# Softmax of neighbourhood attention fused differently, and weight sums of the v and g projections moved from accumulating DMAs to GpSimd, in a two-layer encoder

## The chip, the cores and the metric

One core of a Trainium2 chip. The metric is the device time of one execution in microseconds (us). Engines: TensorE (PE; weight loads PEld), VectorE (DVE), ScalarE (ACT), GpSimd (POOL), SyncE (SP, which here only issues DMAs).

## The reference, cut to what matters

Two layers over 512 tokens (8 rows of 64 columns) of width 1024, all float32. Each layer: one input projection of x to neighbourhood attention (8 heads of 64), retention (4 heads, q and k of 128, v and g of 256) and gates; then a merge, LayerNorm, a gated feed-forward part and a second LayerNorm. The change lies in the neighbourhood attention and in the projection to v and g:

```python
s = einsum('bhcd,bhrckd->bhcrk', q_row, k_win) * scale   # window: 8 rows x 16 columns
s = s + bias                                             # na_rpb at row and column offset
pr = softmax(s over the window's 128 keys)
out = einsum('bhcrk,bhrckd->bhcd', pr, v_win)
...
proj = x @ w_in[i]      # q_na, k_na, v_na, q_r, k_r, v_r, g_r, gate_a, gate_b
yb = silu(g_r) * groupnorm(retention(q_r, k_r, v_r))
```

## The kernel before, in words

**Matmuls.** Every float32 product is three matmuls on a split operand: `hi` is the value cast to fp32r on ScalarE, `lo` is value minus `hi` on VectorE (`split`, lines 157 and 158; `mm3`, lines 372 to 374). Each weight goes through this: a DMA brings 128x1024 (`raw`, 512 KB), ScalarE makes `hi`, VectorE `lo`, TensorE uses both. `Stream` holds all weights of the program in the order of use; `load` runs `LOOK` = 3 items ahead of `prep` (the split), which runs ahead of `get` (the use).

**The v/g stage.** The columns of v and g are done in two blocks of two heads (0 and 1). In a block the weight is cut into quarters a, b, c, d, and seven products in place of eight are formed, with the sums t1 = a+b, t2 = t1+d, t4 = t2+c and t3 = b+d of packed quarters (the signs are in the packing). `block_items` makes the items a, c, t1, t2, d, t3, t4, two halves each. The raw buffer of a becomes that of t1, t2 and t4 in turn (`nxt`): once one is split, `Stream.add` adds the next quarter to the raw tile (`rawa`) by a GpSimd DMA with accumulation from DRAM. t3 (`rawt`) is loaded as b, with d added in the same way, when the item d is loaded (`early`). So for t2 and t3 the same quarter d is read from DRAM again, besides its own load for the product d. `VG0` and `VG1` give the order of products by hand, with other projections (ga0 to ga3, q0, k0) and, in layer 0, the start-up work between them; `vg_sums` makes the corresponding sums of x (tiles s, sh, sl) on VectorE. GpSimd otherwise issues the accumulating DMAs of other stages, raises variances to the power -0.5, and little else.

**The attention stage.** After v/g, the remaining projections (`FILL`) and gates run as fillers on TensorE, one slot each; retention heads and neighbourhood heads are generators whose steps are put between the fillers by slot numbers (`RET_AT`, `NA_AT`). The framework then orders each engine's instructions; each engine works through its own queue in order. `na_head(h)` has three steps. First step: the window of biases `tb` (128x249) is loaded and, with the mask (0 or -1e30, `mask_sb`), makes the bias B of 128x512, one half for the three inner query tiles, one for the edge tile (line 941); four pairs of matmuls per head give the scores `ns` in two PSUM banks of two query tiles; VectorE adds B into S (lines 958 and 961), takes the maximum over each of the four tiles at once (963), negates it (964); ScalarE does four exponentials with the sum (967); VectorE the reciprocal (970) and four scales (972). Second step: eight transposes of S on TensorE (980) and their split (`pt`). Third: matmuls with `vn`, the split v (992), and copies. `vn` is made by `na_v`, a filler which stands between the heads, from `xc`, a reordered copy of x made on ScalarE (`column_tiles`, line 892) just before.

**Buffers.** `up` is the pool of units of 4 KB per partition that hold S, split operands, raw tiles of a and t3 and much else; there are `N_UNIT` = 27. Plain raw tiles come from a pool of three.

Of the kernel before, what the change touches and what calls it, by code (L numbers as in the profile page):

```python
# [8 lines left out]
F32 = mybir.dt.float32  # L9
F32R = mybir.dt.float32r  # L10
AF = mybir.ActivationFunctionType
ALU = mybir.AluOpType
# [9 lines left out]
LN_EPS = 1e-5  # L22
GN_EPS = 1e-6
ALPHA = (2.0 * DEPTH) ** 0.25
RPB_PAD = 16
RPB_N = 8 * 15 * 31

N_UNIT = 27
N_RAW = 3
N_W = 3  # L30
N_TMP = 6
# [69 lines left out]
    return a.bitcast(F32)  # L101


def trunk(tc, wpack, x_nat, x_tr, head, p_tr, rpb, decay, ln_par, ln_col, conv, cos_t, sin_t, dist, xi_d, zd, mask, ident_d, out):
    nc = _Engines(tc)
    _Ordered.on = set()
    from contextlib import ExitStack
# [1 line left out]
    with ExitStack() as es:  # L109
# [14 lines left out]
        def nm(s):  # L124
            cnt[0] += 1
            return f"{s}_{cnt[0]}"
# [21 lines left out]
        mask_sb = cp.tile([P, 512], F32, name="mask_sb")  # L148
        cos_sb = cp.tile([P, 512], F32, name="cos_sb")
        sin_sb = cp.tile([P, 512], F32, name="sin_sb")  # L150

# [8 lines left out]
        class Item:  # L160
# [7 lines left out]
            def __init__(self, kind, src, width, pool=None, plus=None, own=None):  # L168
                self.kind, self.src, self.width, self.pool, self.plus, self.own = kind, src, width, pool, plus, own
                self.raw = self.hl = None  # L170
                self.nxt = self.early = self.block = None

                self.sent = kind == "w" and any(a <= src[1] < b for a, b in SENT)

        def block_items(pos, held, early):

            out = []
            prev = {}
            for kind, src, plus in (("a", "a", None), ("c", "c", None), ("t1", None, "b"), ("t2", None, "d"),
                                    ("d", "d", None), ("t3", "b", "d"), ("t4", None, "c")):  # L180
                for j in range(2):
                    at = lambda q: None if q is None else pos[q, j]
                    it = Item(kind, at(src), pos["a", j][3], plus=at(plus), own=kind in ("a", "t3"), pool=held.get(kind))
                    if kind in ("a", "t1", "t2", "t4"):
                        if j in prev:
                            prev[j].nxt = it
                        prev[j] = it
                    if kind == "t3":
                        [o for o in out if o.kind == early][j].early = it
                    out.append(it)  # L190
            return out

        def down_items(l, s):
# [16 lines left out]
        def vg_items(l):  # L210

            by = {}
            for b in range(2):
                pos = {(q, j): (l, 12 * b + 2 * i + j, 0, 1024) for i, q in enumerate("acbd") for j in range(2)}
                for it in block_items(pos, {k[1:]: up for k in VG_HELD[l] if k[0] == str(b)}, VG_EARLY):
# [34 lines left out]
        class Stream:  # L250
# [26 lines left out]
                self.late = {}  # L277

            def add(self, it):
                l, c, o, w = it.plus  # L280
                nc.gpsimd.dma_start(it.raw[:, :w], wpack[l, c][:, o:o + w], accum_op=ALU.add)

# [16 lines left out]
            def load(self, n, part=None):  # L299

                while self.nload < min(n, len(self.seq)):
                    it = self.seq[self.nload]
                    if it.src is not None and it.kind != "t3":
                        self.fetch(it, part)
                        if it.early is not None:
                            self.fetch(it.early)
                    self.nload += part != 0
                    if part == 0:
                        return
# [224 lines left out]
        def tables():  # L534
            for t, d in ((cos_sb, cos_t), (sin_sb, sin_t), (xi_sb, xi_d.to_broadcast([P, 512])), (dist_sb, dist), (ident, ident_d)):
                nc.sync.dma_start(t, d)
            yield
            nc.sync.dma_start(mask_sb, mask)
            for h in range(2):
                tbs[0, h] = bp.tile([P, 249], F32, tag="tb", name=nm("tb"))  # L540
# [82 lines left out]
        for l in range(DEPTH):  # L623
# [307 lines left out]

            def na_head(h):
                m, rr = h // 2, (h % 2) * 64
                tb = tbs.pop((l, h), None)
                if tb is None:
                    tb = bp.tile([P, 249], F32, tag="tb", name=nm("tb"))
                    nc.sync.dma_start(tb, rpb[l, h])
                B = bp.tile([P, 512], F32, tag="B", name=nm("B"))
                for o, off, st in ((0, 0, 16), (256, 8, 0)):
                    v3 = lambda x: x[:, o:o + 256].rearrange("p (b r j) -> p b r j", b=2, j=16)  # L940
                    nc.vector.tensor_add(v3(B), _ap(tb, off, [[st, 2], [31, 8], [1, 16]]), v3(mask_sb))
                S = unit_f("S")
                q, k, kw = qn[m], kn[m], kl[m]
                hs = slice(rr, rr + 64)

# [3 lines left out]
                for b in range(2):  # L949
                    ps = bank("ns")  # L950
                    for gi in range(2):
                        g = 2 * b + gi
                        c = slice(g * P, (g + 1) * P)
                        o = ps[:, gi * 256:(gi + 1) * 256]
                        nc.tensor.matmul(o, q[:, h % 2, c], kv(k[:, h % 2, :], g), start=True, stop=False)
                        nc.tensor.matmul(o, q[:, h % 2, c], kv(kw[:, h % 2, :], g), start=False, stop=True)
                    if b == 0:
                        nc.vector.tensor_add(S[:, 0:512].rearrange("p (g n) -> p g n", g=2), ps.rearrange("p (g n) -> p g n", g=2),
                                             _ap(B, 0, [[0, 2], [1, 256]]))
                    else:  # L960
                        nc.vector.tensor_add(S[:, 512:1024], ps, B)
                nmx = small("nmx", 4)
                nc.vector.tensor_reduce(nmx, S.rearrange("p (g n) -> p g n", g=4), axis=AX.X, op=ALU.max)
                nc.vector.tensor_scalar_mul(nmx, nmx, -1.0)
                sm = small("sm", 4)
                for g in range(4):
                    nc.scalar.activation(S[:, g * 256:(g + 1) * 256], S[:, g * 256:(g + 1) * 256], AF.Exp,
                                         bias=nmx[:, g:g + 1], accum_out=sm[:, g:g + 1])
                rc = small("rc", 4)
                nc.vector.reciprocal(rc, sm)  # L970
                for g in range(4):
                    nc.vector.tensor_scalar_mul(S[:, g * 256:(g + 1) * 256], S[:, g * 256:(g + 1) * 256], rc[:, g:g + 1])
# [555 lines left out]

def _rpb_windows(rpb):

    flat = np.pad(rpb.reshape(DEPTH, RPB_N), ((0, 0), (RPB_PAD, RPB_PAD)))
    h = np.arange(8)[:, None, None, None] * 465
    rq = np.arange(8)[None, :, None, None]
    u = np.arange(16)[None, None, :, None]
    idx = RPB_PAD + h + (7 - rq) * 31 + 7 - u + np.arange(249)
    return flat[:, idx.reshape(8, P, 249)]


def _consts():
    half = 64  # L1540
    f = np.float32
    inv = (f(10000.0) ** (-np.arange(half, dtype=f) / f(half))).astype(f)
    ang = np.arange(T, dtype=f)[None, :] * inv[:, None]
    cos, sin = np.cos(ang).astype(f), np.sin(ang).astype(f)
    cos_t = np.concatenate([cos, cos], 0)
    sin_t = np.concatenate([sin, -sin], 0)
    dist = (np.arange(384)[None, :] - np.arange(P)[:, None] - 128).astype(f)
    n = np.arange(T)
    xi = np.where(n < 256, 256 - n, n - 255).astype(f)[None, :]
    zd = np.where(n < 256, 255 - n, n - 256).astype(f).reshape(4, P).T  # L1550
    u = np.arange(P) % 16
    j = np.arange(32)
    vi = (j[None, :] - u[:, None] >= 0) & (j[None, :] - u[:, None] < 16)
    ve = (j[None, :] // 16) == (u[:, None] // 8)
    mk = lambda v: np.tile(np.where(v, 0.0, -1e30).astype(f).reshape(P, 2, 1, 16), (1, 1, 8, 1)).reshape(P, 256)
    mask = np.concatenate([mk(vi), mk(ve)], 1)
    return cos_t, sin_t, dist, xi, zd, mask, np.eye(P, dtype=f)


# [36 lines left out]
```

## Time and profile before

| what | value |
|---|---|
| time, median of 3 runs | 1695.96 us (1695.86 to 1696.27) |
| the profiled execution: span, first to last instruction | 1694.1 us, granted TensorE clock 0.998 |
| median less span (start and end around the instructions) | 1.9 us |
| PE busy | 1680.6 us (99%), 7895 matmuls |
| DVE, ACT, POOL busy | 1227.8 (72%), 923.8 (55%), 146.7 us (9%) |
| moved by DMA | 256.59 MB, mean 151 GB/s |

The profiled execution's own time is its span. In rows of groups the columns are line, engine, operation, output<-inputs, shape, count, then busy us and mean ns of one, then the engine's idle time just before them and what ended it. In rows of the timeline they are start (us), duration (us; of the whole run of instructions where the row has x2 or more), engine, line, operation, names, count, and in brackets idle time with its releaser.

### The profile page before, as it was taken

The page shows a single profiled execution, that of the slowest core. Times are in us where ns is not written, and L with a number is a line of the kernel's source. Part 1 is how long each engine was busy: PE and PEld are TensorE (multiplying, and loading weights), DVE is VectorE, ACT ScalarE, POOL GpSimd, SP SyncE. Part 2 cuts the span into 40 slices and gives each one's busy share as a digit, 9 for nine tenths or more (in the row PEclk, how much of TensorE's full clock was granted, in tenths as well). Part 3 has the DMA queues.
Part 4 walks back from the last instruction along what each step waited for, and adds up shares of the span by engine and source line. Part 5 has one row for each costly group of instructions (what it writes and reads, how often), then busy time and mean ns, then how long its engine had stood idle before and what let it go on. Part 6 is the DMA issues. An engine that isn't in the chain of part 4 may idle for free.

```text
span 1694.1 us, 21018 instructions
## 1 busy us (share of the span) xinstructions
PE 1680.6 (99%) x7895; PEld 1404.1 (83%) x7895; DVE 1227.8 (72%) x1848; ACT 923.8 (55%) x1368; POOL 146.7 (9%) x166
## 2 busy tenths in 40 slices
PE   9999999999999999999999999999999999999997
PEld 7888888888888888888888888888888888888886
DVE  6667767756787767757876677576578887676678
ACT  6755668654367445344476555676534574353452
POOL 1100010000200100100112001100002010000003
PEclk9999999999999999999999999999999999999999
DMA  8954464344655535535779435643456565264275
GB/s 299 259 160 131 112 155 110 108 143 147 190 148 151 123 113 164 136 111 173 201 206 238 124 98 133 150 103 106 147 203 188 135 173 125 88 185 126 87 212 100
DMA packets 76855, 256.59 MB, mean 151 GB/s; under 512 B 8912, under 2 KB 11472, under 8 KB 76752
## 3 DMA queue, kind: packets, MB, share of 16 engines
q1 hardware_dynamic: 58608, 191.27, 32.8%
q0 software_dynamic: 18144, 63.97, 21.7%
q8 instruction: 62, 1.02, 0.2%
q14 instruction: 41, 0.34, 0.1%
HBM read 240.53 MB, written 13.63 MB: 150 GB/s over the span
## 4 chain that ended last, share of the span: by engine, by line
PE 97%; DVE 2%; ACT 1%; issue 0%; DVEq 0%; ACTq 0%
PE gt L87 32%; PE u L87 13%; PE gt L372 8%; PE gt L373 8%; PE gt L374 8%; PE v L87 7%; PE w L87 3%; PE gn L372 3%; PE gn L374 3%; PE gn L373 3%; PE x L87 2%; PE gn L87 1%; PE na L992 1%; PE pt L980 1%; PE o L374 1%; PE o L373 1%
## 5 line engine op out<-in xcount | busy, mean ns | idle before, releaser
L87 PE MATMUL gt<-x1t,hi 128*128 128x512 f32 x1408 | 433.3, 389 | 0.0
L87 PEld LDWEIGHTS gt<-x1t,hi 128*128 128x128 f32 x1408 | 264.3, 188 | 54.6
L87 PE MATMUL gt<-x1t,lo 128*128 128x512 f32 x704 | 274.1, 389 | 0.1
L87 DVE TENSOR_TENSOR lo<-raw,hi 128x1024 fp32r<-128x1024 f32 (+1 forms) x155 | 185.6, 1208 | 45.0 <-ACT hi L87 44.6
L87 DVE SCALAR_TENSOR_TENSOR ca<-gt,cw,ca 128x511 f32<-128x511 f32 x176 | 131.8, 749 | 79.1 <-ACT ca L87 75.6
L87 ACT CAST hi<-raw 128x1024 fp32r<-128x1024 f32 (+1 forms) x155 | 159.3, 1038 | 35.8 <-PE u L87 16.6
L372 PE MATMUL gt<-xt,hi 128*128 128x512 f32 x416 | 163.5, 393 | 0.0
L373 PE MATMUL gt<-xt,hi 128*128 128x512 f32 x416 | 162.2, 390 | 0.0
L374 PE MATMUL gt<-xt,lo 128*128 128x512 f32 x416 | 162.1, 390 | 0.0
L87 PEld LDWEIGHTS gt<-x1t,lo 128*128 128x128 f32 x704 | 132.2, 188 | 28.4 <-DVE lo L87 1.0
L157 ACT CAST hi<-raw 128x1024 fp32r<-128x1024 f32 x72 | 75.6, 1050 | 126.4 <-PE gt L373 65.4
L87 ACT ACTIVATE ca<-gt,cw 128x512 f32<-128x512 f32 x88 | 68.6, 779 | 131.9 <-PE gt L87 131.9
L87 DVE TENSOR_TENSOR lo<-rawa,hi 128x1024 fp32r<-128x1024 f32 x90 | 104.7, 1175 | 42.3 <-ACT hi L87 42.0
L158 DVE TENSOR_TENSOR lo<-raw,hi 128x1024 fp32r<-128x1024 f32 x72 | 88.0, 1222 | 62.4 <-ACT hi L157 62.1
L87 ACT CAST hi<-rawa 128x1024 fp32r<-128x1024 f32 x90 | 90.0, 1013 | 38.3 <-DMA rawa<-in_wpack 19.9
L374 PEld LDWEIGHTS gt<-xt,lo 128*128 128x128 f32 x416 | 78.1, 188 | 16.6
L87 POOL DMA_DIRECT2D rawa<-in_wpack x68 | 61.3, 916 | 338.2 <-DVE lo L87 293.5
L373 PEld LDWEIGHTS gt<-xt,hi 128*128 128x128 f32 x416 | 78.3, 188 | 14.9
L372 PEld LDWEIGHTS gt<-xt,hi 128*128 128x128 f32 x416 | 78.2, 188 | 14.9
L87 PE MATMUL gt<-xt,hi 128*128 128x512 f32 x192 | 59.1, 389 | 0.0
L87 PE MATMUL v<-hi,sa 128*128 128x512 f32 x176 | 56.1, 389 | 0.0
L372 PE MATMUL gn<-hi,mt 128*128 128x512 f32 x128 | 50.2, 392 | 0.0
(324 smaller groups left out, 3600.0 us busy)
## 6 DMA issues: line engine op xcount, KB each, us to landing
raw<-in_wpack SPq DMA_DIRECT2D x247, 512.0 KB, 3.9
rawa<-in_wpack POOLq DMA_DIRECT2D x66, 512.0 KB, 6.3
lo<-in_wpack POOLq DMA_DIRECT2D x24, 512.0 KB, 6.7
rawa<-in_wpack SPq DMA_DIRECT2D x22, 512.0 KB, 6.5
rawt<-in_wpack SPq DMA_DIRECT2D x22, 512.0 KB, 6.8
rawt<-in_wpack POOLq DMA_DIRECT2D x22, 512.0 KB, 7.6
r_scr<-pp SPq DMA_DIRECT2D x8, 512.0 KB, 10.0
g_scr<-sga SPq DMA_DIRECT2D x16, 256.0 KB, 4.0
```

Source lines behind the costliest of these rows:

```text
L87: r = f(*a, **k)
L157: nc.scalar.copy(hi, src)
L158: nc.vector.tensor_sub(lo, src, _f(hi))
L372: nc.tensor.matmul(ps, lh, rh, start=start, stop=False, skip_group_check=more)
L373: nc.tensor.matmul(ps, lh, rl, start=False, stop=False, skip_group_check=more)
L374: nc.tensor.matmul(ps, ll, rh, start=False, stop=stop, skip_group_check=more)
L980: nc.tensor.transpose(ps[:, i * P:(i + 1) * P], S[:, g * 256 + bb * P:g * 256 + (bb + 1) * P], ident)
L992: nc.tensor.matmul(ov[kt], lv, pt[kt // 2][:, sp_, c], start=i == 0 and sp_ == 0, stop=i == 3 and sp_ == 1)
```

## The change

1. In `na_head`, B (bias and mask together, 128x512) comes ready from DRAM: the host's gather puts -1e30 where the mask was. `tb`, `mask_sb` and line 941 go.
2. The two S adds, the maximum and the negation become four fused instructions of 128x256 (one per query tile): S = -(scores + B), with the running minimum as accumulator into `nmx`. The exponential takes scale -1.
3. The four scales by the reciprocal move from VectorE to ScalarE (a Copy with a scale per partition).
4. In the two v/g blocks of both layers, t2 and t3 get d by a GpSimd add of 128x1024 from d's own raw tile, which is now loaded with the first of them that needs it, into a unit buffer (`own`), in place of the accumulating DMA. t1 and t4 keep their DMAs.
5. 30 unit buffers instead of 27, and a scratch area for GpSimd's DMA descriptors of 4096 bytes per partition in place of the default.

```diff
-N_UNIT = 27
+N_UNIT = 30
...
-        def block_items(pos, held, early):
+        def block_items(pos, held, early, onchip=False):
...
+            if onchip:
+                ds = [o for o in out if o.kind == "d"]
+                for it in out:
+                    if it.kind == "d":
+                        it.own = True
+                    if it.kind in ("t2", "t3"):
+                        it.other = ds[len([o for o in out[:out.index(it)] if o.kind == it.kind])]
...
             def add(self, it):
+                if it.other is not None:
+                    if it.other.raw is None:
+                        self.fetch(it.other)
+                    nc.gpsimd.tensor_tensor(it.raw, it.raw, it.other.raw, ALU.add)
+                    return
                 l, c, o, w = it.plus
                 nc.gpsimd.dma_start(it.raw[:, :w], wpack[l, c][:, o:o + w], accum_op=ALU.add)
...
                     if it.src is not None and it.kind != "t3":
-                        self.fetch(it, part)
+                        if it.raw is None or part is not None:
+                            self.fetch(it, part)
...
-                tb = tbs.pop((l, h), None)
-                if tb is None:
-                    tb = bp.tile([P, 249], F32, tag="tb", name=nm("tb"))
-                    nc.sync.dma_start(tb, rpb[l, h])
-                B = bp.tile([P, 512], F32, tag="B", name=nm("B"))
-                for o, off, st in ((0, 0, 16), (256, 8, 0)):
-                    v3 = lambda x: x[:, o:o + 256].rearrange("p (b r j) -> p b r j", b=2, j=16)
-                    nc.vector.tensor_add(v3(B), _ap(tb, off, [[st, 2], [31, 8], [1, 16]]), v3(mask_sb))
+                B = tbs.pop((l, h), None)
+                if B is None:
+                    B = bp.tile([P, 512], F32, tag="B", name=nm("B"))
+                    nc.sync.dma_start(B, rpb[l, h])
...
-                    if b == 0:
-                        nc.vector.tensor_add(S[:, 0:512].rearrange("p (g n) -> p g n", g=2), ps.rearrange("p (g n) -> p g n", g=2),
-                                             _ap(B, 0, [[0, 2], [1, 256]]))
-                    else:
-                        nc.vector.tensor_add(S[:, 512:1024], ps, B)
-                nmx = small("nmx", 4)
-                nc.vector.tensor_reduce(nmx, S.rearrange("p (g n) -> p g n", g=4), axis=AX.X, op=ALU.max)
-                nc.vector.tensor_scalar_mul(nmx, nmx, -1.0)
+                    for gi in range(2):
+                        g = 2 * b + gi
+                        nc.vector.tensor_tensor_reduce(S[:, g * 256:(g + 1) * 256], ps[:, gi * 256:(gi + 1) * 256],
+                                                       B[:, 0:256] if g < 3 else B[:, 256:512], -1.0, 3e38,
+                                                       ALU.add, ALU.min, nmx[:, g:g + 1])
...
-                                         bias=nmx[:, g:g + 1], accum_out=sm[:, g:g + 1])
+                                         bias=nmx[:, g:g + 1], scale=-1.0, accum_out=sm[:, g:g + 1])
...
-                    nc.vector.tensor_scalar_mul(S[:, g * 256:(g + 1) * 256], S[:, g * 256:(g + 1) * 256], rc[:, g:g + 1])
+                    nc.scalar.activation(S[:, g * 256:(g + 1) * 256], S[:, g * 256:(g + 1) * 256], AF.Copy, scale=rc[:, g:g + 1])
...
-    nc = bacc.Bacc("TRN2", target_bir_lowering=False, num_devices=1)
+    nc = bacc.Bacc("TRN2", target_bir_lowering=False, num_devices=1, dynamic_dma_scratch_size=4096)
```

The matmuls are the same 7895. Moved with the rest in the compiled order: at head 0 of each layer one xc cast stands ahead of the table load and the exponentials on ScalarE, with a hi cast now behind them; a group of vn matmuls is six matmuls later on TensorE; B loads and some raw loads change places on SP.

More of the change, by code (lines that the diff above doesn't have):

```diff
@@ L24 @@
 ALPHA = (2.0 * DEPTH) ** 0.25
-RPB_PAD = 16
-RPB_N = 8 * 15 * 31
-N_UNIT = 27
+N_UNIT = 30
 N_RAW = 3
@@ L101, in _f, with trunk @@
     return a.bitcast(F32)
-def trunk(tc, wpack, x_nat, x_tr, head, p_tr, rpb, decay, ln_par, ln_col, conv, cos_t, sin_t, dist, xi_d, zd, mask, ident_d, out):
+def trunk(tc, wpack, x_nat, x_tr, head, p_tr, rpb, decay, ln_par, ln_col, conv, cos_t, sin_t, dist, xi_d, zd, ident_d, out):
     nc = _Engines(tc)
@@ L147, in trunk @@
         zd_sb = cp.tile([P, 4], F32, name="zd_sb")
-        mask_sb = cp.tile([P, 512], F32, name="mask_sb")
         cos_sb = cp.tile([P, 512], F32, name="cos_sb")
@@ L170, in __init__ @@
                 self.raw = self.hl = None
-                self.nxt = self.early = self.block = None
+                self.nxt = self.early = self.block = self.other = None
                 self.sent = kind == "w" and any(a <= src[1] < b for a, b in SENT)
-        def block_items(pos, held, early):
+        def block_items(pos, held, early, onchip=False):
             out = []
@@ L214, in vg_items @@
                 pos = {(q, j): (l, 12 * b + 2 * i + j, 0, 1024) for i, q in enumerate("acbd") for j in range(2)}
-                for it in block_items(pos, {k[1:]: up for k in VG_HELD[l] if k[0] == str(b)}, VG_EARLY):
+                for it in block_items(pos, {k[1:]: up for k in VG_HELD[l] if k[0] == str(b)}, VG_EARLY, True):
                     it.block = b
@@ L537, in tables @@
             yield
-            nc.sync.dma_start(mask_sb, mask)
             for h in range(2):
-                tbs[0, h] = bp.tile([P, 249], F32, tag="tb", name=nm("tb"))
+                tbs[0, h] = bp.tile([P, 512], F32, tag="B", name=nm("B"))
                 nc.sync.dma_start(tbs[0, h], rpb[0, h])
@@ L933, in na_head @@
                 m, rr = h // 2, (h % 2) * 64
-                tb = tbs.pop((l, h), None)
-                if tb is None:
-                    tb = bp.tile([P, 249], F32, tag="tb", name=nm("tb"))
-                    nc.sync.dma_start(tb, rpb[l, h])
-                B = bp.tile([P, 512], F32, tag="B", name=nm("B"))
-                for o, off, st in ((0, 0, 16), (256, 8, 0)):
-                    v3 = lambda x: x[:, o:o + 256].rearrange("p (b r j) -> p b r j", b=2, j=16)
-                    nc.vector.tensor_add(v3(B), _ap(tb, off, [[st, 2], [31, 8], [1, 16]]), v3(mask_sb))
+                B = tbs.pop((l, h), None)
+                if B is None:
+                    B = bp.tile([P, 512], F32, tag="B", name=nm("B"))
+                    nc.sync.dma_start(B, rpb[l, h])
                 S = unit_f("S")
+                nmx = small("nmx", 4)
                 q, k, kw = qn[m], kn[m], kl[m]
@@ L1529, in _rpb_windows @@
 def _rpb_windows(rpb):
[L1531 to L1536, printed above, removed]
+    u = np.arange(P) % 16
+    rq = np.arange(P) // 16
+    b, r, j = np.arange(2)[:, None, None], np.arange(8)[None, :, None], np.arange(16)[None, None, :]
+    pad = np.full((DEPTH, 8, 1), -1e30, rpb.dtype)
+    flat = np.concatenate([rpb.reshape(DEPTH, 8, -1), pad], axis=2)
+    row = (r[None] + 7 - rq[:, None, None, None]) * 31
+    off = 16 * b + j
+    uu = u[:, None, None, None]
+    inner = np.where((off - uu >= 0) & (off - uu < 16), row + 7 + off - uu, flat.shape[2] - 1)
+    edge = np.where(b == uu // 8, row + 15 + j - uu, flat.shape[2] - 1)
+    idx = np.stack(np.broadcast_arrays(inner, edge), axis=1).reshape(P, 512)
+    return flat[:, :, idx]
 def _consts():
@@ L1550, in _consts @@
     zd = np.where(n < 256, 255 - n, n - 256).astype(f).reshape(4, P).T
[L1551 to L1557, printed above, removed]
+    return cos_t, sin_t, dist, xi, zd, np.eye(P, dtype=f)
 def kernel(x, p, w_in, na_rpb, ret_decay_f, ret_decay_b, w_branch_a, w_branch_b, w_out,
@@ L1569 @@
         w_down, w_ple_gate, w_ple_proj, ln2_g, ln2_b))
-    cos_t, sin_t, dist, xi, zd, mask, ident = _consts()
+    cos_t, sin_t, dist, xi, zd, ident = _consts()
     xx = x.reshape(T, D)
@@ L1585 @@
         "conv": np.concatenate([conv_w, conv_b[:, None]], 1).reshape(DEPTH, 4, 2 * NF, P).transpose(0, 3, 2, 1),
-        "cos_t": cos_t, "sin_t": sin_t, "dist": dist, "xi": xi, "zd": zd, "mask": mask, "ident": ident,
+        "cos_t": cos_t, "sin_t": sin_t, "dist": dist, "xi": xi, "zd": zd, "ident": ident,
     }
     arr = {k: np.ascontiguousarray(v) for k, v in arr.items()}
-    nc = bacc.Bacc("TRN2", target_bir_lowering=False, num_devices=1)
+    nc = bacc.Bacc("TRN2", target_bir_lowering=False, num_devices=1, dynamic_dma_scratch_size=4096)
     args = [nc.dram_tensor(f"in_{k}", v.shape, F32, kind="ExternalInput").ap() for k, v in arr.items()]
```

## The prediction, as put on record

> **What bounds the kernel now.** I read the page first: the busy times and the chain.
>
> ```profile
> span 1694.1 us, 21018 instructions
> PE 1680.6 (99%) x7895; PEld 1404.1 (83%) x7895; DVE 1227.8 (72%) x1848; ACT 923.8 (55%) x1368; POOL 146.7 (9%) x166
> PE 97%; DVE 2%; ACT 1%; issue 0%; DVEq 0%; ACTq 0%
> ```
>
> TensorE is busy for 1680.6 of 1694.1 us, and is 97% of the chain. The change takes no matmul away, so it can only fill TensorE's idle time: 1694.1 - 1680.6 = 13.5 us. Where that lies, the waits of TensorE and the timeline's end tell.
>
> ```profile
> PE warm L475 <- DVE warm L472: 1.2, 1, 1.2
> PE gn L372 <- ACT xc L892: 1.0, 2, 0.5
> PE gt L87 <- DVE lo L87: 0.5, 2, 0.3
> ```
>
> ```profile
> 1680.22 3.33 PE L87 MATMUL x<-xw,k 128*128 128x512 f32 x14
> ```
>
> The columns of the waits are total, times, longest. The last matmul ends at 1680.22 + 3.33 = 1683.55, and 10.55 us of normalisation and output follow; 1.2 us is the wait of the warm-up at the start. The change touches neither. That leaves 13.5 - 10.55 - 1.2 = 1.75 us in the middle. A matmul is counted 0.39 us while the next starts after 0.23, so each stall is really about 0.16 longer than shown, and stalls below 0.16 are not seen. With about seven places (the four counted above, one before S is transposed, two that the view does not list), the ceiling of any gain is 1.75 + 7 x 0.16 = 2.9 us. **That is less than 0.2% of the time (3.4 us)**, about what a measurement of this kernel can tell from no change; I use it as the bound below. Losses have no such ceiling, so the rest of the argument is on whether the change makes TensorE wait. The stages concerned (first neighbourhood attention of either layer, then v/g of either layer) are as full as the rest, at a granted clock of 1.00:
>
> ```profile
> 250.00:385.00 135.00, 134.42 (x696) 113.89 (x695) 89.52 (x170) 85.45 (x160) 3.17 (x4) 1.00 0.42 122
> 1090.00:1226.00 136.00, 135.49 (x703) 115.05 (x702) 93.67 (x171) 86.66 (x161) 3.82 (x5) 1.00 0.39 118
> 16.00:127.00 111.00, 110.83 (x495) 91.66 (x494) 79.46 (x116) 73.53 (x100) 15.02 (x17) 1.00 0.81 225
> 868.00:968.00 100.00, 99.69 (x447) 82.45 (x445) 65.27 (x78) 64.06 (x89) 11.35 (x13) 1.00 0.68 180
> ```
>
> Columns: stretch, length, then busy time of PE, weight loads, DVE, ACT, POOL, clock, DMA share, GB/s. VectorE works about 70% of each stage and ScalarE about 63%, so throughput of neither is the issue; order and lateness of single instructions are.
>
> **The attention part.** Prices of what goes, by groups of instructions (busy us, mean ns; in the two rows with colons least, median and most ns):
>
> ```profile
> L941 DVE TENSOR_TENSOR B<-tb,mask_sb 128x256 f32<-128x256 f32 x32 | 12.8, 416 | 0.0
> L958 DVE TENSOR_TENSOR S<-ns,B 128x512 f32<-128x512 f32 x16 | 10.9, 682 | 0.0
> L963 DVE TENSOR_REDUCE nmx<-S 128x4 f32<-128x1024 f32 x16 | 19.5, 1219 | 0.5
> L972 DVE TENSOR_SCALAR S<-S,rc 128x256 f32<-128x256 f32 x64 | 18.3, 350 | 0.5
> L964 DVE TENSOR_SCALAR nmx<-nmx x16: 158/164/170, 254.0 to 1201.6; 128x4 f32<-128x4 f32 x16
> L970 DVE RECIPROCAL rc<-sm x16: 178/178/180, 258.3 to 1203.9; 128x4 f32<-128x4 f32 x16
> L967 ACT ACTIVATE S<-S,nmx 128x256 f32<-128x256 f32 x64 | 31.8, 499 | 8.2 <-DVE nmx L964 8.1
> L830 ACT ACTIVATE kz<-kz,zeta 128x128 fp32r<-128x128 f32 x32 | 11.6, 361 | 6.5 <-DVE kz L831 6.4
> ```
>
> Per head VectorE loses 2 x 0.42 (bias plus mask), 2 x 0.68 (S), 1.22 (maximum), 0.16 (negate) and 4 x 0.35 (scale): 5.0 us. It gains four fused instructions. No row shows one: the lower end is the two-input 128x256 add, 0.42; the upper end is that add plus a quarter of the maximum, 0.42 + 0.30 = 0.72, and 0.16 for a small instruction that reads out the accumulator, 0.9. I take 0.5, near the row with the same operands: 2.0 us. Relief 3 us per head, 48 in all, on an engine that bounds nothing. ScalarE gains four scales per head, between the 128x128 row with a scale per partition (0.36) and the 128x256 exponential (0.50); I take 0.45: 1.8 us per head, 29 in all; by the windows ScalarE has some 50 us free in 135.
>
> The chain of one head gets shorter. Before, from the second S add: 0.68 + 1.22 + 0.16, four exponentials at 0.5, reciprocal 0.2 and four scales at most 0.35 each, 5.6 us. After: two fused instructions (1.0), the last exponential (0.5, the others run while the scores come), reciprocal 0.2, scales 1.8, 3.5 us. So S is ready about 2 us earlier for its transposes, also where that was short:
>
> ```profile
> 366.76 0.64 PEld L980 LDWEIGHTS pt<-ident,S 128*128 128x128 f32 x6 [0.31 <-DVE S L972]
> ```
>
> That stall (about 0.24 us of TensorE) goes. So do the two largest. At 258 TensorE wants xc, and ScalarE has first a table load, four exponentials, and a cast before them:
>
> ```profile
> 253.79 1.05 ACT L330 CAST hi<-raw 128x1024 fp32r<-128x1024 f32 x1 [3.42 <-PE gt L373]
> 254.86 1.28 ACT L967 ACT_TABLE_LOAD   x1
> 258.14 1.12 ACT L892 CAST xc<-xt 128x512 fp32r<-128x512 f32 x2
> 258.01 0.28 PE L374 MATMUL o<-su,qx 128*128 128x256 f32 x1
> 258.80 0.50 PE L372 MATMUL gn<-hi,xc 128*128 128x512 f32 x1 [0.51 <-ACT xc L892]
> ```
>
> From 258.01 to 258.80 is 0.79 where 0.12 is the pitch: 0.67 lost, and the same in layer 1. In the changed order one xc cast stands ahead of the table load, and the 1.05 us cast stands behind. Removed: 2 x 0.67 + 0.24 = **1.6 us**.
>
> What is late next is vn in head 2. In the new order ScalarE has the four exponentials behind the first vn cast and the four scales behind the second, and VectorE has the reciprocal, which waits for all exponentials, ahead of its vn splits. Before:
>
> ```profile
> 281.88 0.68 DVE L958 TENSOR_TENSOR S<-ns,B 128x512 f32<-128x512 f32 x1
> 284.42 0.59 ACT L157 CAST vn<-gn 128x512 fp32r<-128x512 f32 x1 [0.72 <-PE gn L374]
> 285.83 0.59 ACT L157 CAST vn<-gn 128x512 fp32r<-128x512 f32 x1 [0.82 <-PE gn L374]
> 284.80 0.68 DVE L158 TENSOR_TENSOR vn<-gn,vn 128x512 fp32r<-128x512 f32 x1
> 286.45 0.69 DVE L158 TENSOR_TENSOR vn<-gn,vn 128x512 fp32r<-128x512 f32 x1 [0.30 <-ACT vn L157]
> 285.54 0.30 PEld L992 LDWEIGHTS na<-pt,vn 128*128 128x128 f32 x2 [0.22 <-DVE vn L158]
> 287.20 0.77 PEld L992 LDWEIGHTS na<-pt,vn 128*128 128x128 f32 x6 [0.21 <-DVE vn L158]
> ```
>
> The second split ends at 285.48 and is loaded at 285.54; the fourth ends at 287.14 and is loaded at 287.20: no slack in either. Afterwards the fused instructions start at the S add's place, 281.88; the four exponentials (2 us from about 282.4) put the second vn cast at 284.4, its split at 285.0 to 285.7: 0.2 late. The fourth follows reciprocal and scales (284.8 to 286.6), so cast at about 287.1 and split until 288.4; but the new order of TensorE has six more matmuls ahead of that group (6 x 0.23 = 1.4), so it is wanted at about 288.6. Between 0.2 and 0.6 us lost per layer; I take 0.4: **+0.8 us** in both layers. With the fused instruction at 0.9 instead of 0.5, 1.6 us more stands ahead of the vn splits and some 1.4 per layer more is lost.
>
> The loads that change with it: mask (256 KB, once) and 16 windows of 128 KB give way to 16 of 256 KB, which queue on SP ahead of weights. The DMA share there is 0.42 and 0.39, which hides them; uncovered, another 128 KB at the 122 GB/s shown is 1 us.
>
> **The v/g part.** Sixteen of the accumulating DMAs (t2 and t3 of two blocks, two halves, two layers) become GpSimd adds of 128x1024; the transfers fall by 16 x 512 KB. What the rows show of such an add, and of what it does to VectorE:
>
> ```profile
> L87 POOL TENSOR_TENSOR R<-R,lng 128x1024 f32<-128x1024 f32 x2 | 5.1, 2554 | 0.7 <-ACT R L87 0.7
> rawa<-in_wpack POOLq DMA_DIRECT2D x66, 512.0 KB, 6.3
> ```
>
> ```profile
> 1681.01 2.70 POOL L87 TENSOR_TENSOR R<-R,lng 128x1024 f32<-128x1024 f32 x1
> 1682.64 2.15 DVE L87 SCALAR_TENSOR_TENSOR R<-R,mv,lng 128x1024 f32<-128x1024 f32 x1
> 1687.82 1.28 DVE L87 SCALAR_TENSOR_TENSOR R<-R,mv,lng 128x1024 f32<-128x1024 f32 x1
> ```
>
> A sum takes 2.55 instead of 6.3 us to landing, so t2 and t3 are whole sooner. But while GpSimd ran until 1683.71, a VectorE instruction with two SBUF inputs took 2.15; the same form alone took 1.28. It gave up 0.87 of the 1.07 us that it lay beside GpSimd. The Trainium skill, "SBUF — State Buffer", section "Who interferes with whom", states this as a rule: a VectorE instruction with two SBUF inputs and a GpSimd instruction that reads SBUF exclude each other, and the first to start keeps the port for its whole length; the rows above agree. Every lo split (raw and hi, both in SBUF, 1.22 us) is of that form. The tight place is block 0 of layer 0:
>
> ```profile
> 56.90 1.22 DVE L87 TENSOR_TENSOR lo<-raw,hi 128x1024 fp32r<-128x1024 f32 x1 [1.71 <-ACT hi L87]
> 58.43 1.23 DVE L87 TENSOR_TENSOR lo<-raw,hi 128x1024 fp32r<-128x1024 f32 x1 [0.30 <-ACT hi L87]
> 60.97 0.39 PE L87 MATMUL gt<-xt,lo 128*128 128x512 f32 x1
> ```
>
> The split ends at 59.66 and is used at 60.97: 1.3 us of slack. The t3 adds fall about there. If one gets the port ahead of that split, it ends at 59.66 + 2.55 = 62.2: 1.25 us lost; if VectorE comes first, nothing. Both are about as likely; I take half, **+0.6 us**. Elsewhere I cost the adds at nothing: VectorE's idle time covers them, 31.5 of 111 us in layer 0 and 34.7 of 100 in layer 1; what they cost without that cover is rival (b). SP loads the d quarter earlier, into unit buffers (30 instead of 27); the DMA share of 0.81 and 0.68 falls with the reads, which covers this. If a weight came late because of that order, one 512 KB load (about 4 us) would be the price.
>
> **The sum,** against the profiled execution: 1694.1 - 1.6 + 0.8 + 0.6 = 1693.9 us of span. The median lies 1.9 us above the span (1695.96 - 1694.1), for what lies around it; so 1695.96 - 0.2, **1695.8 us**.
>
> **The rivals.**
> (a) Everything late is hidden, and the small stalls go too: -1.6 to -2.9, 1693.1 to 1694.4. For it: the chain of a head is 2 us shorter, and sums are there sooner. Against it: vn has no slack at 285.54. Within 0.2%. Chance 0.2.
> (b) **Slower:** GpSimd's adds exclude VectorE's splits in every block. Place: the lo splits of the v/g stage; price per block 2.55 less a slack between the 1.3 above and an estimated 0.5, so 1.25 to 2.05; over four blocks 5.0 to 8.2, with the -0.8 of the attention part 1700.2 to 1703.4. It decides from the point where an add starts less than about 2.5 us ahead of a split whose slack is under 2.5. For it: the row of 2.15. Against it: that only one place in my walk through the stage is that tight. Chance 0.18.
> (c) The fused instruction takes 0.9 or more, and vn comes 2 x 1.4 later: 1698.6, still within 0.2%; with twice that beyond it. Chance 0.12, a third of it beyond.
> (d) The change doesn't do what it says: the sums or the scales wait behind something else in their queues, and the old stalls stay while the new ones come: +1.4, 1697.4. Chance 0.08.
> The forecast itself, 1694.6 to 1697.2, has 0.42.
>
> **The numbers.** Faster by over 0.2% needs more than the ceiling: 0.04, taken from the forecast, for what I have not seen at the start or the end. Slower: (b) 0.18 and a third of (c): 0.22. Same: 0.74. The range goes from the lower end of (a) to the lower part of (b), 1693.1 to 1701.
>
> **What would show it.** TensorE's waits: xc gone from the list, a wait for vn of 0.2 to 0.6 per layer in its place, a wait for lo near 61 us if the adds exclude the splits; lo splits of 2 us or more next to GpSimd adds of 2.5; a fused instruction near 0.5; TensorE's busy time unchanged. The forecast is wrong if lo waits appear in all four blocks, if the fused instruction takes over 0.9, or if TensorE waits for raw loads.

## The result and the profile after

The changed kernel takes 1701.07 us (median of 9 runs, 1699.73 to 1701.47) against 1696.27 (9 runs, 1695.86 to 1696.87): ratio 1.0026, 95% interval 1.0016 to 1.0036. It is slower by 4.8 us, just past the upper end of the range, 1701. The profiled execution took 1699.88 us, its span is 1697.9, 3.8 above that of before.

The page's head of the changed kernel, and what TensorE waited for (total, times, longest):

```profile
span 1697.9 us, 21017 instructions
PE 1681.9 (99%) x7895; PEld 1404.5 (83%) x7895; DVE 1207.3 (71%) x1816; ACT 948.7 (56%) x1432; POOL 175.3 (10%) x166
```

```profile
PE gt L84 <- ACT hi L84: 2.7, 2, 1.6
PE gt L84 <- DVE lo L84: 1.6, 4, 0.5
PE warm L484 <- DVE warm L481: 1.2, 1, 1.2
```

The wait for xc has left the list. In its place stands a wait for a ScalarE cast, once in each layer, that was in no list before, and two more waits for lo behind it. Following the same matmul through both traces shows where the spans part (negative: earlier than before):

| place | shift, us |
|---|---|
| start, before the first loop of real matmuls settles | +0.84 |
| v/g, layer 0: block 0, block 1 | +2.21, +0.22 |
| attention, layer 0 | -1.21 |
| the rest of layer 0 | +0.09 |
| v/g, layer 1: block 0, block 1 | +2.68, +0.24 |
| attention, layer 1 | -0.97 |
| the rest, to the last instruction | -0.30 |
| sum | +3.80 |

So the attention part won 2.2 us and the v/g part lost 5.4. This is block 0 of layer 0 on GpSimd, VectorE, ScalarE and TensorE:

```profile
53.86 2.70 POOL L84 TENSOR_TENSOR rawt<-rawt,rawd 128x1024 f32<-128x1024 f32 x1
56.29 1.09 POOL L84 DMA_DIRECT2D rawa<-in_wpack  x1
56.90 2.91 POOL L84 TENSOR_TENSOR rawt<-rawt,rawd 128x1024 f32<-128x1024 f32 x1
```

```profile
54.01 6.36 DVE L84 SCALAR_TENSOR_TENSOR s<-s,xf 128x512 f32<-128x512 f32 x1
```

The same sums in the kernel before:

```profile
51.04 1.29 DVE L87 SCALAR_TENSOR_TENSOR s<-s,xf 128x512 f32<-128x512 f32 x2
```

And again in the changed kernel:

```profile
60.40 1.22 ACT L84 CAST sh<-s 128x512 fp32r<-128x512 f32 x2 [6.79 <-DVE s L84]
61.53 1.04 ACT L84 CAST hi<-raw 128x1024 fp32r<-128x1024 f32 x1
```

```profile
61.13 0.39 PE L84 MATMUL u<-hi,sl 128*128 128x512 f32 x1
62.62 0.73 PE L84 MATMUL gt<-xt,hi 128*128 128x512 f32 x2 [1.10 <-ACT hi L84]
63.88 0.50 PE L84 MATMUL gt<-xt,lo 128*128 128x512 f32 x1 [0.53 <-DVE lo L84]
```

Read it from the top. GpSimd's two t3 adds run from 53.86 to 59.81. VectorE starts s, a sum of two SBUF tiles, at 54.01, and it lasts 6.36 us; before, two of them took 1.29. It ends 0.56 us after the second add. ScalarE is idle for 6.79 us, waiting for s; its queue holds the cast of the next weight behind the cast of s, so `hi` of ga2 comes at 61.53 to 62.57. TensorE waits, first for `hi`, then for `lo`. Neither `raw` nor the matmuls that wait had anything to do with s: the two casts only share ScalarE's queue.

### The profile page after: what moved, and what is told of

It reads as the page before. It is cut to its first block, busy times and chain, and to the rows that moved or that the text cites. A ratio compares the mean times of both kernels' runs of the same rounds, so it can differ in the third digit from the quotient of the medians.

```text
span 1697.9 us, 21017 instructions
## 1 busy us (share of the span) xinstructions
PE 1681.9 (99%) x7895; PEld 1404.5 (83%) x7895; DVE 1207.3 (71%) x1816; ACT 948.7 (56%) x1432; POOL 175.3 (10%) x166
## 4 chain that ended last, share of the span: by engine, by line
PE 97%; DVE 2%; ACT 1%; issue 0%; DVEq 0%; ACTq 0%
PE gt L84 32%; PE u L84 13%; PE gt L382 8%; PE gt L381 8%; PE gt L383 8%; PE v L84 7%; PE w L84 3%; PE gn L383 3%; PE gn L382 3%; PE gn L381 3%; PE x L84 2%; PE gn L84 1%; PE na L994 1%; PE pt L982 1%; PE o L383 1%; PE o L382 1%
## 5 line engine op out<-in xcount | busy, mean ns | idle before, releaser
L84 ACT CAST hi<-raw 128x1024 fp32r<-128x1024 f32 (+1 forms) x147 | 151.2, 1037 | 32.7 <-PE u L84 14.9
L84 POOL DMA_DIRECT2D rawa<-in_wpack x60 | 54.4, 926 | 267.0 <-DVE lo L84 236.2
```

The lines of the kernel that those rows point to most:

```text
L84: r = f(*a, **k)
```

## The experiments

Theory A: GpSimd's t3 adds shut VectorE's s out, and ScalarE's queue hands the delay on to the weights. Theory B: the attention part costs the time (its scales on ScalarE, its bigger bias loads). A third question was the start.

**The parts apart.** The first kernel takes the GpSimd adds out of the change:

```diff
-                for it in block_items(pos, {k[1:]: up for k in VG_HELD[l] if k[0] == str(b)}, VG_EARLY, True):
+                for it in block_items(pos, {k[1:]: up for k in VG_HELD[l] if k[0] == str(b)}, VG_EARLY):
```

> The changed kernel with the sums t2 and t3 back on accumulating DMAs; attention part, 30 units and scratch size stay. Theory A (GpSimd's t3 adds shut VectorE's sums of x out, and ScalarE's hi cast stands behind them in its queue): the 2.2 and 2.7 us in block 0 of v/g vanish, attention keeps its gain of about 1.2 us per layer, so about 1694 to 1695.5, below the kernel before. Theory B (the attention part, its scales on ScalarE or the bigger bias loads cost the time): still 1699 to 1701. Theory C (the 0.84 us at the start, from the order of loads, belongs to this part): TensorE's start stays late by 0.8.

Measured 1693.30 us (1695.68 before on that chip): 0.9985, interval 0.9976 to 0.9994. The start is not late in its trace (0.06 us earlier than before), so theory C, the third question's, falls too. The second has the adds, units and scratch size without the attention part (items 4 and 5 of the change on the kernel before):

> The kernel before with the GpSimd adds, 30 units and the scratch size, and the old attention part. Theory A: all of the loss and none of the gain, 1696.3 + 4.9 to 6.5, so 1701 to 1703, with TensorE waiting for hi near 61 and 903 us. Theory B: no loss, 1696.

Measured 1702.17: 1.0042, 1.0029 to 1.0054. The third has item 5 alone:

```diff
-N_UNIT = 27
+N_UNIT = 30
...
-    nc = bacc.Bacc("TRN2", target_bir_lowering=False, num_devices=1)
+    nc = bacc.Bacc("TRN2", target_bir_lowering=False, num_devices=1, dynamic_dma_scratch_size=4096)
```

> The kernel before with 30 units and the scratch size alone. Theory A: nothing, 1696.0 to 1696.6. Rival: more units let raw loads run earlier on SP and collide at the start, +0.8, 1697.

Measured 1694.90: 0.9994, 0.9985 to 1.0003. Theory A holds so far and B falls: the loss is in the adds, and what the first kernel keeps is worth 2.4 us. What I had not expected is that item 5 alone also loses the wait for xc. Its waits, warm-up aside, and two rows of ScalarE:

```profile
PE gt L87 <- DVE lo L87: 0.5, 2, 0.3
```

```profile
251.40 1.14 ACT L892 CAST xc<-xt 128x512 fp32r<-128x512 f32 x2
254.82 1.28 ACT L967 ACT_TABLE_LOAD   x1
```

Two casts to xc now stand ahead of the table load, probably as more buffers let the framework place them there; the scratch size changed with them. Is the gain then the units' and not the attention part's? The attention part alone, with 27 units:

```diff
-N_UNIT = 30
+N_UNIT = 27
```

> The kernel before with the changed attention part alone: no GpSimd adds, 27 units (the scratch size stays). If the gain at xc comes from the attention part, 1693.3 to 1694.5, as with 30 units. If it comes from the units (30 units alone lost the xc wait too), the wait for xc is back and 1694.5 to 1695.9.

Measured 1693.29 (1695.85): 0.9983, 0.9974 to 0.9992, the same as with 30. Either edit takes the xc wait away, they don't add up there, and the attention part takes more besides. This is the version that beats both kernels. Its waits, warm-up aside, are one line, that of before:

```profile
PE gt L84 <- DVE lo L84: 0.5, 2, 0.3
```

**The scales.** The kernel of the first experiment with the scales back on VectorE:

```diff
-                    nc.scalar.activation(S[:, g * 256:(g + 1) * 256], S[:, g * 256:(g + 1) * 256], AF.Copy, scale=rc[:, g:g + 1])
+                    nc.vector.tensor_scalar_mul(S[:, g * 256:(g + 1) * 256], S[:, g * 256:(g + 1) * 256], rc[:, g:g + 1])
```

> The changed kernel without GpSimd adds, and with the four scales of each head back on VectorE. If the scales on ScalarE cost anything (vn later, 0.17 us per layer), this is 0.2 to 0.4 faster than 1693.3; if VectorE is what S waits for at its transposes, 0.2 to 0.5 slower.

Measured 1695.13 (1695.85): 0.9995, 0.9986 to 1.0005, some 1.8 us more than with ScalarE's scales. More than either expected, and at another place: not S but vn is late. The four scales now stand in VectorE's queue ahead of the second vn split, and the first group of vn matmuls waits for it, once in each layer:

```profile
283.51 1.14 DVE L974 TENSOR_SCALAR S<-S,rc 128x256 f32<-128x256 f32 x4
284.57 1.88 DVE L154 TENSOR_TENSOR vn<-gn,vn 128x512 fp32r<-128x512 f32 x3
285.30 0.51 PE L994 MATMUL na<-pt,vn 128*128 128x256 f32 x2 [0.71 <-DVE vn L154]
```

**Which adds.** Only t2 on GpSimd, then only t3 (the condition in `block_items`, cut to one kind):

```diff
-                    if it.kind in ("t2", "t3"):
+                    if it.kind in ("t2",):
```

> The changed kernel with t3 back on accumulating DMAs; only t2 is summed by GpSimd. Theory A (the two t3 adds shut out VectorE's sum s, so ScalarE's casts behind it are late): no wait for hi near 61 and 903 us, about 1693.3 to 1694.5, as with no GpSimd add at all. Rival (any add costs, or the t2 adds that stretch vl from 1.30 to 4.33 us): half of the loss stays, 1696 to 1698.

> The changed kernel with t2 back on accumulating DMAs; only t3 is summed by GpSimd. Theory A: the whole loss stays, waits for hi near 61 and 903 us, 1699 to 1701.5. Rival: half of it, 1696 to 1698.

Measured 1694.62 and 1694.65 (1695.88): 0.9992, 0.9982 to 1.0001, and 0.9994, 0.9984 to 1.0003. **Theory A failed here**: t3 alone was to carry the whole loss; neither kernel has a wait for hi, and TensorE loses nothing in block 0 of either layer. (Both kernels are still some 1.3 us above the one without adds. In their profiles block 1 costs about 0.25 us per layer; the rest is not traced to the adds.) The t3-only trace shows the difference:

```profile
54.35 2.39 POOL L84 TENSOR_TENSOR rawt<-rawt,rawd 128x1024 f32<-128x1024 f32 x1 [2.82 <-DMA rawt<-in_wpack]
56.69 0.87 POOL L84 DMA_DIRECT2D rawa<-in_wpack  x1
59.17 3.17 POOL L84 TENSOR_TENSOR rawt<-rawt,rawd 128x1024 f32<-128x1024 f32 x1 [1.61 <-DMA rawt<-in_wpack]
```

```profile
52.80 1.30 DVE L84 TENSOR_TENSOR sl<-s,sh 128x512 fp32r<-128x512 f32 x2
54.35 3.46 DVE L84 TENSOR_TENSOR lo<-raw,hi 128x1024 fp32r<-128x1024 f32 x1 [0.26 <-ACT hi L84]
57.74 2.35 DVE L84 TENSOR_TENSOR lo<-rawd,hi 128x1024 fp32r<-128x1024 f32 x2
60.01 3.48 DVE L84 TENSOR_TENSOR s<-xf,xf 128x512 f32<-128x512 f32 x2
```

Here each add waits for its own load, they start 4.8 us apart, and VectorE gets three splits in between. In the changed kernel both loads have long landed, and both adds stand in GpSimd's queue behind the t2 work: they run in one go. The new theory, A2: it takes two adds in a row. If so, one of the two is harmless even with t2 on GpSimd:

```diff
-                    if it.kind in ("t2", "t3"):
-                        it.other = ds[len([o for o in out[:out.index(it)] if o.kind == it.kind])]
+                    j = len([o for o in out[:out.index(it)] if o.kind == it.kind])
+                    if it.kind == "t2" or it.kind == "t3" and j == 0:
+                        it.other = ds[j]
```

> The changed kernel with t2 and the first half of t3 summed by GpSimd, the second half of t3 by an accumulating DMA. Theory A2 (the loss needs two t3 adds back to back, between which VectorE does not get the port): s is held up by one add, 2.7 us instead of 5.7, the slack covers most of it, so 1693.8 to 1696. Rival A3 (t2 adds together with any t3 add do it): 1698 to 1701.

Measured 1694.33 (1695.85): 0.9991, 0.9982 to 1.0000. A2 holds for the t3 adds: s lasts 3.11 us, and the wait for hi is gone.

```profile
53.52 3.11 DVE L84 SCALAR_TENSOR_TENSOR s<-s,xf 128x512 f32<-128x512 f32 x1
```

That two adds follow each other is not enough, though. In the changed kernel the two t2 adds stand next to each other, with nothing between them, and VectorE gets in:

```profile
41.09 3.31 POOL L84 TENSOR_TENSOR rawa<-rawa,rawd 128x1024 f32<-128x1024 f32 x1 [16.21 <-DVE lo L84]
44.36 2.84 POOL L84 TENSOR_TENSOR rawa<-rawa,rawd 128x1024 f32<-128x1024 f32 x1
```

```profile
43.42 1.53 DVE L84 TENSOR_TENSOR vl<-p,vh 128x512 fp32r<-128x512 f32 x1
44.87 2.88 DVE L84 TENSOR_TENSOR vl<-p,vh 128x512 fp32r<-128x512 f32 x1
```

The first vl (two SBUF inputs, like s) waits for the first add, which ends at 44.40, and is done at 44.95, early in the second add; the second vl waits for the second add alone. All nine profiles with whole or halved t2 adds show it, in block 0 of both layers. The t3 adds differ in that a DMA issue of GpSimd stands right ahead of each (56.29 in the changed kernel). Their records differ too: the record behind a t2 add starts 0.03 to 0.05 us before the add ends, the one behind a t3 add of the changed kernel 0.26 us or more. Which of these makes the two t3 adds act as one, no run separates.

**When VectorE gets in.** Each add cut into halves:

```diff
-                    nc.gpsimd.tensor_tensor(it.raw, it.raw, it.other.raw, ALU.add)
+                    for i in range(2):
+                        nc.gpsimd.tensor_tensor(it.raw[:, i * 512:(i + 1) * 512], it.raw[:, i * 512:(i + 1) * 512],
+                                                it.other.raw[:, i * 512:(i + 1) * 512], ALU.add)
```

> The changed kernel with each GpSimd add cut into two of 128x512. If the port is held for one whole instruction, a waiting VectorE instruction gets it between two halves: s (two instructions) is delayed by about 3 us instead of 5.7, which the slack nearly covers, so 1693.5 to 1696. If GpSimd keeps the port as long as its queue has adds, nothing changes: 1700 to 1701.5.

Measured 1701.53: 1.0033, 1.0021 to 1.0046; nothing gained. One s now lasts 6.62 us, over the four halves of t3 (between those of t2 VectorE gets in):

```profile
53.65 6.62 DVE L84 SCALAR_TENSOR_TENSOR s<-s,xf 128x512 f32<-128x512 f32 x1
```

Then s and its split one product earlier, so that it is done before the adds:

```diff
-... "0t1": [sums], "ga1": [sums], "ga2": [sums ...
+... "0t1": [sums, sums], "ga2": [sums ...
```

> The changed kernel with the third sum of x (s and its split sl) put one product earlier, ahead of the t3 adds. Theory A: s is no longer shut out, the stall of 2.2 and 2.7 us goes; what the t3 adds then hold up are lo splits with more slack, so 1693.5 to 1697. Rival: the t3 adds hold up the next instruction with two SBUF inputs and TensorE waits as long: 1699 to 1701.5.

Measured 1698.09: 1.0013, 1.0004 to 1.0023, between the two expectations. The next instruction with two SBUF inputs is shut out in place of s, now the lo split itself, and only the detour through ScalarE is saved. TensorE loses 1.9 us in each layer, not 2.2 and 2.7, and in this profile the granted clock stays at 1.00 behind the stall (the last run below shows why that counts):

```profile
56.27 6.31 DVE L84 TENSOR_TENSOR lo<-raw,hi 128x1024 fp32r<-128x1024 f32 x1 [0.51 <-ACT hi L84]
```

Last, GpSimd instructions that read nothing from SBUF ahead of each t3 add, one or three memsets of 128x512:

```diff
+                    if it.kind == "t3":
+                        for _ in range(1):   # 3 in the second kernel
+                            nc.gpsimd.memset(gap, 0.0)
                     nc.gpsimd.tensor_tensor(it.raw, it.raw, it.other.raw, ALU.add)
```

> The changed kernel with one GpSimd memset of 128x512, which reads nothing from SBUF, ahead of each t3 add. If VectorE misses the port only because the next add starts right behind, it gets it during the memset: s ends about 2.5 us sooner, the stalls near 61 and 903 us nearly go, 1694 to 1697. If GpSimd keeps the port over whatever stands in its queue, s is later by the memsets: 1701 to 1703.

> The same with three memsets ahead of each t3 add, so a gap of a few us. If a gap of any length lets VectorE in: as with one, 1694 to 1697, with t3 late by the memsets. If only a gap longer than some limit does: faster than with one. If none does: 1703 to 1708.

One memset: 1703.38 (1695.78), 1.0043, 1.0028 to 1.0058, worse than none. Three: 1694.95, 0.9994, 0.9985 to 1.0004. The wait for hi is gone although GpSimd does more. With one, then with three:

```profile
53.86 2.70 POOL L84 TENSOR_TENSOR rawt<-rawt,rawd 128x1024 f32<-128x1024 f32 x1
56.78 1.15 POOL L84 MEMSET gap<- 128x512 f32 x1
57.27 3.00 POOL L84 TENSOR_TENSOR rawt<-rawt,rawd 128x1024 f32<-128x1024 f32 x1
```

```profile
53.54 7.29 DVE L84 SCALAR_TENSOR_TENSOR s<-s,xf 128x512 f32<-128x512 f32 x1
```

```profile
54.95 2.53 POOL L84 TENSOR_TENSOR rawt<-rawt,rawd 128x1024 f32<-128x1024 f32 x1
58.02 1.98 POOL L84 MEMSET gap<- 128x512 f32 x3
59.97 2.59 POOL L84 TENSOR_TENSOR rawt<-rawt,rawd 128x1024 f32<-128x1024 f32 x1
```

```profile
53.15 1.29 DVE L84 SCALAR_TENSOR_TENSOR s<-s,xf 128x512 f32<-128x512 f32 x2
54.52 3.51 DVE L84 TENSOR_TENSOR sl<-s,sh 128x512 fp32r<-128x512 f32 x2
57.95 1.21 DVE L84 TENSOR_TENSOR lo<-raw,hi 128x1024 fp32r<-128x1024 f32 x1
```

With one memset the adds are 0.71 us apart (56.56 to 57.27), and the waiting s still does not get in. With three, two things change. The memsets ahead of the first add delay it, so that s is done (54.44) before the add starts (54.95): that alone spares s. And the adds are 2.49 us apart (57.48 to 59.97): the waiting sl gets in right behind the first add and ends at 58.03, with a lo split after it. So VectorE does not get in across a gap of 0.71 us here, does across one of 2.49, and does without a gap between the t2 adds: the length of the gap is not what decides by itself. Behind the first t3 add with three memsets, the next record starts 0.04 us before its end, as behind a t2 add; with one memset 0.36 us. In all the profiles VectorE gets in where that overlap is 0.05 us or less, and not where it is 0.24 us or more and another add follows. That is a sign, not a cause; the cause stays open. (In the kernel with one memset s starts 0.32 us ahead of the first add's record and is shut out all the same; the records of GpSimd overlap each other by as much, so they don't tell who asked first.)

**The adds on VectorE:**

```diff
-                    nc.gpsimd.tensor_tensor(it.raw, it.raw, it.other.raw, ALU.add)
+                    nc.vector.tensor_tensor(it.raw, it.raw, it.other.raw, ALU.add)
```

> The changed kernel with the sixteen adds on VectorE (1.22 us each) in place of GpSimd. No exclusion is left; VectorE does 9.8 us more per layer in v/g, where it has some 30 us free. If the loss is the exclusion, 1693.3 to 1695; if it is that the sum stands in the way of VectorE's queue whoever makes it, 1696 to 1700.

Measured 1695.66 (1695.85): 0.9998, 0.9988 to 1.0007, between the two expectations: 2.4 us worse than the DMA sums of the first experiment, 5 to 6 better than GpSimd's. No wait for hi is left, but VectorE's longer queue makes TensorE wait for lo:

```profile
PE u L84 <- DVE lo L84: 1.0, 2, 0.8
```

**The same kernel again.**

> The changed kernel unchanged, for a second profile. Its times lie in two groups, 1699.7 to 1700.4 and 1701.1 to 1701.5, and the profile shown fell in the first. Theory A: in a run of the second group one more VectorE instruction is shut out in v/g, +1.3 us there. Rival: the difference lies at the start, where the first loads land.

Measured 1701.38: 1.0034, 1.0022 to 1.0047. Its profile fell into the upper group of times, and neither expectation fits. The stall at 61 us is as long as in the first profile, but after it TensorE is slow (columns as in the prediction's windows; the granted clock stands ahead of the DMA share):

```profile
60.90:62.60 1.70, 0.63 (x3) 0.21 (x2) 1.45 (x3) 1.70 (x3) 0.41 (x1) 1.00 0.97 137
62.60:64.60 2.00, 1.47 (x6) 0.89 (x6) 1.79 (x2) 2.00 (x3) 0.00 (x0) 1.00 1.02 197
64.60:68.00 3.40, 3.40 (x10) 2.68 (x9) 3.32 (x5) 2.29 (x5) 0.00 (x0) 0.51 0.86 204
68.00:72.00 4.00, 4.00 (x18) 3.21 (x18) 3.05 (x16) 2.83 (x5) 0.00 (x0) 0.99 0.00 0
```

The first profile over the same stretch:

```profile
64.60:68.00 3.40, 3.40 (x17) 2.79 (x16) 3.32 (x5) 2.29 (x5) 0.00 (x0) 1.00 0.96 222
```

Ten matmuls instead of 17 in 3.4 us: the granted clock is halved, which costs 7 x 0.23 = 1.6 us. That is about the distance between the groups of times (1699.7 to 1700.4 at a mean clock of 0.998, 1701.1 to 1701.5 at 0.997). The kernel with the adds alone has it in layer 1 too, at a mean clock of 0.996:

```profile
910.00:913.20 3.20, 3.20 (x9) 2.50 (x8) 2.90 (x5) 2.16 (x3) 0.00 (x0) 0.50 0.03 11
```

## Why the prediction was wrong

**The ceiling** of 2.9 us for any gain held: the best version gains 2.6.

**The attention part** was right in direction and mis-sized. The fused instruction is as I took it:

```profile
L964 DVE CUSTOM_DVE_ANT_0 S<-ns,B 128x256 f32<-128x256 f32 x64 | 23.9, 417 | 0.1
L964 DVE DVE_READ_ACCUMULATOR2_ANT nmx<- 128x1 f32 x64 | 5.3, 82 | 0.0
L974 ACT ACTIVATE S<-S,rc 128x256 f32<-128x256 f32 x64 | 27.3, 498 | 1.0 <-DVE rc L972 1.0
```

0.42 + 0.08 = 0.50 us, predicted 0.5; a scale 0.43 (27.3 us over 64), predicted 0.45. The stalls at xc and before the transposes of S went, as forecast. Two terms were off. vn: +0.4 per layer predicted, 0.12 and 0.16 in the shift of the trace; the split that the first group needs is some 0.1 us late, and the six matmuls ahead of the second group cover its split wholly. And the stalls that went were larger than reckoned: 0.79 us at xc in either layer (0.67), 0.35 before the transposes (0.24), and some 0.5 in smaller steps that the sum had left out.

**The v/g part** is where it failed: +0.6 us in the sum, 5.4 in the trace. The step was "If one gets the port ahead of that split, it ends at 59.66 + 2.55 = 62.2: 1.25 us lost; if VectorE comes first, nothing. Both are about as likely; I take half, +0.6 us", with "Elsewhere I cost the adds at nothing" behind it. Three things were wrong in it.
1. It priced one add. The two t3 adds shut VectorE out as one of 5.9 us (e9 against the changed kernel; e7 and e13 show the same). Why these two do and the two t2 adds don't is open. I knew that both t3 adds fell there, from the same rows, and did not ask what is between them.
2. It looked for the damage on the weight split. It came by s, which is off that path, through ScalarE's queue. (A lo split is shut out too, in block 1 of layer 0, for 5.72 us, but that block as a whole lost only 0.22.) I had listed what is queued behind instructions on ScalarE for the attention part, and not for this one.
3. It was not a coin's toss. In both layers and in both profiles of this kernel s starts some 0.15 us behind the first t3 add's record and waits for both adds, 6.36 to 6.38 us; the loss was 2.2 and 2.7 us in the first profile.

Rival (b) had the exclusion, at 0.18, but on the lo splits and one add at a time, with the price spread evenly over four blocks: 5.0 to 8.2. Measured were 5.4, nearly all in the two first blocks, and through s. That the total falls inside its bounds is luck. What carried the time past the range is what neither had: the clock that drops after the stall, 1.6 us in five of the nine runs by their times and mean clocks; the four others lie at 1699.7 to 1700.4, inside it.

**Left open.** The start: seven warm-up matmuls, from the same point on, last longer in the profile of the changed kernel (the second row) than before, and the first real ones with them:

```profile
2.87 2.47 PE L475 MATMUL warm<-warm 128*128 128x512 bf16 x7
```

```profile
2.88 3.19 PE L484 MATMUL warm<-warm 128*128 128x512 bf16 x7
```

That is the 0.84 of the table. In the other profiles the start is between 0.20 earlier and 0.73 later than before, and the changed kernel's second profile has 0.59, so it is no property of the change that I could show. Some profiles also lose 0.1 to 1.5 us near 825 us, behind an accumulating DMA of the stage before, with and without GpSimd adds; it was not pursued.

## What to carry to other kernels

Work given to GpSimd is not free because GpSimd idles: here a VectorE instruction with two SBUF inputs that came up beside a GpSimd add waited for it, and in the worst place for two adds as if they were one. Before moving such work, write down what arrives in GpSimd's queue together, which VectorE instruction falls into it, and what stands behind that instruction's consumer on ScalarE. In a kernel whose TensorE is 99% busy, the whole prize was 2.9 us, and one stall of 2 us could cost another 1.6 through the clock.

## What the runs showed of the hardware that I had not expected

- A VectorE sum of two SBUF tiles, 0.65 us alone, lasted 6.36 us beside two GpSimd adds, 6.62 beside four half adds and 7.29 with a memset between two adds. The Trainium skill, "SBUF — State Buffer", section "Who interferes with whom", says that whoever issues first gets the pair for the whole instruction; the t2 adds agree with that (vl waits for one add at a time), the t3 adds do not: there VectorE stayed shut out for the whole run of GpSimd instructions, across a gap of 0.71 us.
- An instruction with one input can wait too: a TENSOR_SCALAR of 128x16 (dl), 0.17 us before, lasted 1.41 us beside a t2 add of the changed kernel (76.29 to 78.69) and ended 0.04 us behind it.
- GpSimd waits too, but for one instruction: in the t3-only kernel its add took 2.39 where it came first (54.35), and 3.17 where a lo split of VectorE was still running until 60.09 (59.17).
- After 1.6 us without matmuls within 3.7 us (60.9 to 64.6), the granted clock was 0.51 for the next 3.4 us in one profile and 1.00 in another with the same stall. The Trainium skill, "TensorE: Matmul & The Clock Gate", section "What's actually happening", gives a free-running window of about 3.4 us and an idle window as the cause of the half rate; the length of the drop agrees, and so does its dependence on chance, but here pauses of 1.6 us in all, by the profile's busy times, with matmuls between them, sufficed.
- A descriptor scratch of 4096 bytes per partition instead of the default, with three more units, came with no loss: 1694.90 us against 1695.68 for the kernel before. No run changes the scratch alone.
